# Layer 1's output product on float16 parts for 24 of 32 steps, with scales from squares summed ahead

## The chip, the cores and the metric

The kernel runs on one core of a Trainium2 chip. The core has TensorE (PE: matmuls, with weight loads shown apart as PEld), VectorE (DVE), ScalarE (ACT), GpSimd (POOL) and SyncE (SP, which here only issues DMAs). Each engine takes its instructions in order from its own queue; semaphores tie the queues together. DMAs are issued from the queues of SyncE, GpSimd and, rarely, ScalarE. The metric is the device time of one execution in microseconds, as the median of several runs.

## The reference

A two-layer transformer-like model on 256 tokens and 256 context tokens, width 2048, branch width 4096, all inputs float32:

```python
for i in range(2):
    shift, scale, gate = split(silu(c) @ ada_w[i] + ada_b[i])
    h  = rmsnorm(x)  * norm_g[i] * (1 + scale)   + shift      # 256 x 2048
    hc = rmsnorm(xc) * norm_g[i] * (1 + scale_c) + shift_c    # context rows
    y, yc = branch[i](h, hc)          # layer 0: Fourier mixer; layer 1: windowed attention
    x = x + gate * (y @ w_out[i])     # (256 x 4096) @ (4096 x 2048)
    if i == 0: xc = xc + gate_c * (yc @ w_out[0])
return rmsnorm(x) * final_g
```

Both branches end in a gate, `f * silu(z)` with `z = h @ w_z`. Layer 1's attention has 64 query heads of width 64 on 8 key/value heads, keys from a window of tokens and from the context. The product that is changed is layer 1's `y @ w_out[1]`, 256 x 4096 by 4096 x 2048.

## The kernel before, in words

**Products from parts.** Every large product is made of three matmuls (`mm3`, lines 144 to 147): each operand is split into a high and a low part, and high x high, high x low and low x high are added in PSUM. The parts have one of two types. On float32r parts, `split` (lines 65 to 67) lets ScalarE cast the source to the high part (L66) and VectorE, or GpSimd, subtract it from the source (L67). On float16 parts, `split16` (L137, L138) multiplies by a power of two first, so that the values fit float16; that scale comes from the sum of the squares of the whole operand (`sum_scale`), and the result is multiplied back by the inverse power. A weight half, 128 x 1024, takes two buffers of the pool `ws` (6 buffers of 4 KB) as float32r and one as float16.

**Layer 0.** After the Fourier mixer (up to about 320 us), z is made on float16 parts for all branch blocks (321 to 658 us, `z_out`). Then comes the output product of layer 0 (659 to 1001 us): 32 steps `i`, two passes (`sw`) over the output's halves with 16 weight tiles (`kg`) each; each step is 48 matmuls of 512 columns. Weights are the held operand, the branch parts stream. Weight tiles with `kg` below 14 use float16, the last two of a pass float32r. The branch parts are made by `y_split0(i + 1)` during step `i`, in the first pass only (the last two pairs in both passes); a float16 part takes the buffer of an earlier branch block, block 0's a buffer of the pool `act`. For the weights' scale, the whole of `w_out[0]` is read a second time ahead of its use, in 128 loads of 256 KB on GpSimd's queue into buffers of `act` (33 of 2 KB), which `scan_loads` issues (L824) and `scan_sums` squares on ScalarE (L817). At the same time VectorE makes the conditioning vectors that come later (`ada_jobs`, L796): a tile of 1 MB of `ada_w` per turn, one or two turns per step (`ada_rate`: two in steps 6 to 9 and 17 to 24). From the output product on, ada tiles and weight tiles share the three buffers of the pool `raw` (L50), loaded on SyncE's queue in the program's order.

**Layer 1.** A short stage ends layer 0 (norms, transposes, stores to `x1d`). The key/value product follows (1007 to 1103 us), on float32r parts, while ScalarE and VectorE make the parts `h1` and `h1c` of the normed rows. Then the attention runs in 66 slots `i` (about 7 us each), with two units of other work in each slot (`filler`, `emit_unit`): the query and z products (units "q" and "z") and at the end 12 units "o", the first 512 columns of the output product for steps k = 0 to 23. A slot has the scores and softmax of one pair of heads (`stage_s`: VectorE L1361 and L1377, ScalarE L1364 and L1376) and the value product of the pair two slots earlier (`stage_o`). Gated branch blocks land in `y1`, two blocks of 256 tokens to a tile (`emit_y`).

**Layer 1's output product.** Tokens are the held operand (two blocks of 128), weights stream 512 wide; 32 steps k. `w1_next` splits a weight half for the first 512 columns (`wo1a`), `y_split` the branch block (ScalarE casts, GpSimd subtracts for k below 24, VectorE above), four steps ahead of use. After the attention come steps 24 to 31 of these columns, then 1024 columns (`wo1b`, 16 tiles) and the last 512 (`wo1c`, 8 tiles). `evac` multiplies by the gate (`gbc`, a row spread over all partitions) and adds the residual, `finish` norms and stores.

**What sets the order.** The program is written once in the order of the loops; a planner then orders each engine's queue by that order and by when it thinks that operands and buffers are ready, so work of later steps runs ahead where its buffers are free. `tc.issue_after(ins)` holds what stands in its block behind `ins` on the same engine. `last_cast` and `last_sub` are the newest cast on ScalarE and subtraction on VectorE (or GpSimd).

## Time and profile before

| | |
|---|---|
| median of 3 runs | 1782.79 us (1778.72 to 1785.88) |
| profiled execution | 1780.77 us |
| its span, first to last instruction | 1779.0 us |
| mean granted TensorE clock | 0.997 |
| busy: PE, PEld, DVE, ACT, POOL | 98%, 69%, 78%, 60%, 16% |
| DMA | 438.74 MB, mean 247 GB/s |

Times in the rows are microseconds from the span's start. The page's second part cuts the span into 40 slices of 44.5 us, one digit each (9 is 90% busy or more). A row of a group by line is: line, engine, operation, tile written and tiles read, shape, count, then busy us and mean ns of one, then the engine's idle time just before such instructions with what ended it. A matmul's duration in the rows overlaps with the next one, so TensorE's pace is read from the count of matmuls in a stretch. In a timeline the bracket has the idle time before an instruction and what it waited for. For a DMA, "to landing" is the time from its issue to its end.

### The profile page before, as it was taken

What the parts mean: (1) busy time and instruction counts of PE and PEld (TensorE: products, weight loads), DVE (VectorE), ACT (ScalarE), POOL (GpSimd) and SP (SyncE); (2) the same over time, 40 slices, a digit from 0 to 9 for tenths busy, and PEclk for the clock granted to TensorE, in tenths of its full rate; (3) what the DMA queues carried; (4) which work ended last, traced back from release to release, by engine and by line L of the source; (5) the groups of instructions that cost most, each with busy time, mean ns of one, the idle gap of its engine ahead of it and who ended that gap; (6) DMA issues with size and microseconds to landing.
All of it is one profiled execution on the core that took longest, in us unless ns stands there. A gap on an engine that the chain in (4) does not pass through costs nothing. (4 is left out here: it accounts for less than half of the span.)

```text
span 1779.0 us, 26403 instructions
## 1 busy us (share of the span) xinstructions
PE 1740.9 (98%) x9517; PEld 1222.3 (69%) x9517; DVE 1392.8 (78%) x2401; ACT 1062.4 (60%) x1989; POOL 293.3 (16%) x368
## 2 busy tenths in 40 slices
PE   6999999999999999999999999999999999999997
PEld 4679999544444444446444888788878888887886
DVE  5779888797777778876885654899899999997455
ACT  5545556377767747544122533688788878896343
POOL 0002111212222132000000000412303230233010
PEclk9999999999999999999999999999999999999999
DMA  9998998778988989774775323588998897987543
GB/s 394 417 357 247 283 276 237 296 285 319 328 305 317 313 302 322 262 298 171 284 287 222 119 95 115 169 193 208 213 209 199 222 217 203 206 210 264 191 167 142
DMA packets 220962, 438.74 MB, mean 247 GB/s; under 512 B 154720, under 2 KB 155120, under 8 KB 189088
## 3 DMA queue, kind: packets, MB, share of 16 engines
q1 hardware_dynamic: 182784, 351.85, 61.0%
q0 software_dynamic: 33904, 78.25, 14.8%
q10 hardware_dynamic: 4144, 6.95, 1.1%
q8 instruction: 75, 1.23, 0.3%
q14 instruction: 55, 0.45, 0.1%
HBM read 391.91 MB, written 12.59 MB: 227 GB/s over the span
## 5 line engine op out<-in xcount | busy, mean ns | idle before, releaser
L67 DVE TENSOR_TENSOR wl<-raw,wh 128x1024 fp32r<-128x1024 f32 x213 | 282.0, 1329 | 144.5 <-ACT wh L66 129.8
L66 ACT CAST wh<-raw 128x1024 fp32r<-128x1024 f32 x213 | 222.4, 1045 | 177.4 <-PE ps L146 152.7
L146 PE MATMUL ps<-act,wf 128*128 128x512 f16 x512 | 194.0, 379 | 0.0
L145 PE MATMUL ps<-act,wf 128*128 128x512 f16 x512 | 189.8, 379 | 1.4 <-ACT act L864 0.7
L147 PE MATMUL ps<-act,wf 128*128 128x512 f16 x512 | 191.1, 379 | 0.0
L1323 PE MATMUL ps<-h,wh 128*128 128x512 f32 x512 | 184.8, 396 | 0.0
L145 PEld LDWEIGHTS <-wf 128*128 128x128 f16 x960 | 94.0, 98 | 118.0 <-ACT wf L137 7.9
L145 PE MATMUL ps<-y,wf 128*128 128x512 f16 x448 | 170.3, 381 | 3.5 <-ACT wf L137 3.5
L147 PEld LDWEIGHTS <-wf 128*128 128x128 f16 x960 | 93.9, 98 | 113.2 <-DVE wf L138 0.3
L146 PE MATMUL ps<-y,wf 128*128 128x512 f16 x448 | 170.8, 381 | 0.0
L146 PEld LDWEIGHTS <-wf 128*128 128x128 f16 x960 | 94.1, 98 | 109.5 <-issue 1.1
L147 PE MATMUL ps<-y,wf 128*128 128x512 f16 x448 | 164.4, 379 | 0.0
L137 ACT ACTIVATE wf<-raw,nrm 128x1024 f16<-128x1024 f32 x56 | 61.3, 1140 | 139.3 <-DMA raw<-in_wo 133.9
L1325 PE MATMUL ps<-h,wl 128*128 128x256 f32 x512 | 138.6, 281 | 0.0
L146 PE MATMUL ps<-wl,h 128*128 128x512 f32 x320 | 126.8, 396 | 0.2 <-DVE wl L67 0.2
L147 PE MATMUL ps<-wh,h 128*128 128x512 f32 x320 | 125.3, 395 | 0.0
L145 PE MATMUL ps<-wh,h 128*128 128x512 f32 x320 | 124.0, 402 | 0.0
L138 DVE SCALAR_TENSOR_TENSOR wf<-raw,tn,wf 128x1024 f16<-128x1024 f32 x64 | 79.8, 1282 | 42.5 <-ACT wf L137 42.4
L1377 DVE SCALAR_TENSOR_TENSOR f<-p,sm,f 128x512 f16<-128x512 f32 x128 | 105.7, 845 | 9.0 <-ACT f L1376 8.6
L1323 PEld LDWEIGHTS ps<-h,wh 128*128 128x128 f32 x512 | 96.3, 188 | 19.0
L1364 ACT ACTIVATE p<-ps,mx 128x512 f32<-128x512 f32 x128 | 87.9, 689 | 35.4 <-DVE mx L1361 30.6
L1376 ACT ACTIVATE f<-p,sm 128x512 f16<-128x512 f32 x128 | 87.6, 717 | 31.8 <-DMA ft<-f 12.9
(394 smaller groups left out, 4452.1 us busy)
## 6 DMA issues: line engine op xcount, KB each, us to landing
raw<-in_wz SPq DMA_DIRECT2D x64, 1024.0 KB, 5.4
raw<-in_adw SPq DMA_DIRECT2D x38, 1024.0 KB, 6.3
raw<-in_awp SPq DMA_DIRECT2D x32, 1024.0 KB, 12.7
act<-in_wo POOLq DMA_DIRECT2D x128, 256.0 KB, 7.2
raw<-in_wo SPq DMA_DIRECT2D x32, 1024.0 KB, 6.7
raw<-in_wq SPq DMA_DIRECT2D x32, 1024.0 KB, 5.2
raw<-in_wu SPq DMA_DIRECT2D x32, 1016.0 KB, 6.6
raw<-in_wo1b SPq DMA_DIRECT2D x16, 1024.0 KB, 4.9
```

Source lines behind the costliest of these rows:

```text
L66: last_cast[0] = S.copy(h, src).ins
L67: last_sub[0] = eng.tensor_tensor(l, src, h.bitcast(F32), op=ALU.subtract).ins
L137: last_cast[0] = S.activation(w[:, 0], src, AF.Copy, scale=up).ins
L138: last_sub[0] = V.scalar_tensor_tensor(w[:, 1], src, up, w[:, 0], op0=ALU.mult, op1=ALU.subtract).ins
L145: PE.matmul(o, wh, xh, start=start, stop=False)
L146: PE.matmul(o, wh, xl, start=False, stop=False)
L147: return PE.matmul(o, wl, xh, start=False, stop=stop).ins
L1323: PE.matmul(o[0], wh[:, q], hx1[k], start=k == 0, stop=k == KT - 1)
L1325: PE.matmul(o[0][:, 0:N], wl[:, q], hx1[k][:, 0:N], start=False, stop=False)
L1364: S.activation(pt[tb], so[tb], AF.Exp, bias=mx[:, tb : tb + 1], scale=-1.0, accum_out=sm[:, tb : tb + 1])
L1376: S.activation(f[:, 0:512], pt[tb], AF.Copy, scale=sm[:, tb : tb + 1])
L1377: V.scalar_tensor_tensor(f[:, 512:1024], pt[tb], sm[:, tb : tb + 1], f[:, 0:512], op0=ALU.mult, op1=ALU.subtract)
```

## The change

Layer 1's output product uses float16 parts for k = 0 to 23, all 2048 columns; k = 24 to 31 stay on float32r.

- The weights' squares: the 24 weight tiles concerned are read a second time in 48 halves. 22 halves are loaded in layer 0's output product from step 14 on (`scan_loads1`, two loads of 256 KB per half on GpSimd's queue into `act`; two halves a step, one in steps 17 to 24) and squared on ScalarE one step later, behind that step's weight casts (`scan_tops1`). 26 halves are loaded in the key/value product (`scan_loads2`, 512 KB each into four new buffers `pz`; four per weight tile, later three).
- The branch's squares: `y_sums` squares each finished tile of `y1` (12 tiles) on ScalarE two slots later. At slots 54 and 56 the sums are joined and the scales made (`out_sum`, `out_scale`).
- Splits: `w_half` makes float16 weight parts. `y_split` works on tiles of two blocks for k below 24: GpSimd multiplies by the scale, ScalarE casts, GpSimd subtracts. Blocks 24 to 31 are multiplied by both scales, so that the sums in PSUM fit together; ScalarE casts and VectorE subtracts, blocks 24 to 27 now inside the loop.
- `gbc` is multiplied by the inverse scale once.
- Layer 0: `y_split0(i + 1)` stands behind the newest weight cast on ScalarE and the newest subtraction on VectorE in all steps, and the ada turns behind the newest subtraction in all steps (before: steps 0, 1 and 12 to 18). The parts of block 1 take a buffer of `act` of their own too.

The diff, cut to its core:

```diff
+    def scan_tops1():
+        while pend:
+            t, c = pend.pop(0)
+            S.activation(t, t, AF.Square, accum_out=c)
+    def scan_loads1(n):
+        for j in [next(scans1) for _ in range(n)]:
+            for q in range(2):
+                t = act()
+                c = (j % 2 * 2 + q) * 512
+                nc.gpsimd.dma_start(t, w1s[j // 2][:, c : c + 512])
...
-                        t = (ypool if k else actp).tile([P, 1024], F16, tag="y" if k else "act", name="y")
+                        t = (ypool if k > 1 else actp).tile([P, 1024], F16, tag="y" if k > 1 else "act", name="y")
...
-            if sw == 0:
+            if i < 14:
...
+            elif i == 14:
+                with tc.issue_after(last_cast[0]):
+                    scan_sums()
+                scan_loads1(2)
+            elif 14 < i < 30:
+                with tc.issue_after(last_cast[0]):
+                    scan_tops1()
+                scan_loads1({i: 1 for i in range(17, 25)}.get(i, 2) if i < 29 else 0)
...
-                y_split0(i + 1)
+                with tc.issue_after(last_cast[0]), tc.issue_after(last_sub[0]):
+                    y_split0(i + 1)
...
-            with tc.issue_after(last_sub[0]) if i < 2 or 11 < i < 19 else nullcontext():
+            with tc.issue_after(last_sub[0]):
                 for _ in range(ada_rate.get(i, 1)):
                     next(ada)
...
+            def scan_loads2(n):
+                for j in [next(scans1) for _ in range(n)]:
+                    t = kvp.tile([P, 1024], F32, tag="pz", name="pz", bufs=4)
+                    nc.gpsimd.dma_start(t, w1s[j // 2][:, j % 2 * 1024 : j % 2 * 1024 + 1024])
+                    pend.append((t, scn[:, j - 22 : j - 21]))
...
+                with tc.issue_after(last_cast[0]):
+                    scan_tops1()
+                with tc.issue_after(pow_end[0]):
+                    scan_loads2(4 if kg < 2 else 3)
...
-                return half_split(raw1[0], n % 2)
+                return (w_half if n < 12 else half_split)(raw1[0], n % 2)
...
+                    S.activation(act(), y1[j], AF.Square, accum_out=g1[:, 2 + j : 3 + j])
...
+            def split16b(h, l, src, up):
+                last_cast[0] = S.activation(h, src, AF.Copy, scale=up).ins
+                last_sub[0] = V.scalar_tensor_tensor(l, src, up, h, op0=ALU.mult, op1=ALU.subtract).ins
...
             def y_split(k):
-                if 16 <= k < 24:
-                    t = act(F32R)
-                else:
-                    t = (h1p if k < 16 else fin[0]).tile([P, 512], F32R, ...)
-                split(t[:, 0:N], t[:, N : 2 * N], y1[k // 2][...], GP if k < 24 else V)
+                src = y1[k // 2]
+                if k < 24:
+                    t = h1p.tile([P, 1024], F16, tag="h1", name="ys", bufs=16)
+                    GP.tensor_tensor(src, src, uy.broadcast_to([P, 512]), op=ALU.mult)
+                    S.copy(t[:, 0:512], src)
+                    GP.tensor_tensor(t[:, 512:1024], src, t[:, 0:512], op=ALU.subtract)
+                    return
...
+            S.activation(gbc, gbc, AF.Copy, scale=dn1)
...
-                w = ws_split(raw(a["wo1b"][kg]))
+                w = [(w_half if kg < 12 else half_split)(t, i) for i in range(2)]
```

More of the change, by code (lines that the diff above doesn't have):

```diff
@@ L1030, in tile_dit @@
                     evac0(sw * 8 + b, o[b])
+    for c, q in ((0, slice(80, 108)), (15, slice(0, 16))):
+        V.tensor_reduce(g1[:, c : c + 1], scn[:, q], axis=AX.X, op=ALU.add)
     x1d = dram.tile([2, P, D], F32, name="x1d")
@@ new lines, in tile_dit, with y_sums, out_sum @@
+            ypairs, ynext = [], [0]
+            def y_sums(n, i):
+                while ynext[0] < min(n, len(ypairs)) and ypairs[ynext[0]] <= i - 2:
+                    j = ynext[0]
+                    ynext[0] += 1
+                    S.activation(act(), y1[j], AF.Square, accum_out=g1[:, 2 + j : 3 + j])
+            uw, uy, ub, dn1 = (g1[:, c : c + 1] for c in (20, 21, 22, 23))
+            def out_sum():
+                V.tensor_reduce(g1[:, 14:15], g1[:, 2:14], axis=AX.X, op=ALU.add)
```

59 lines of the change are left out of this document (49 added, 10 removed).

## The prediction

> **What bounds the kernel now.** I read the page's first two parts, then busy times by stage, then the groups by line.
>
> ```profile
> PE 1740.9 (98%) x9517; PEld 1222.3 (69%) x9517; DVE 1392.8 (78%) x2401; ACT 1062.4 (60%) x1989; POOL 293.3 (16%) x368
> PE   6999999999999999999999999999999999999997
> DVE  5779888797777778876885654899899999997455
> ```
>
> TensorE is busy in every slice from start to end, so a change pays only if TensorE needs less time per product or if one of its few gaps closes; and it costs as soon as another engine makes TensorE wait. VectorE is the only one that comes near, in the attention (slices 26 to 35). The busy time of each stretch (columns: us, then busy time and count of PE, PEld, DVE, ACT, POOL, then granted clock, DMA share, GB/s):
>
> ```profile
> 658.00:700.00 42.00, 42.00 (x196) 19.07 (x195) 34.78 (x52) 25.99 (x53) 13.47 (x25) 1.00 0.95 348
> 734.00:738.00 4.00, 4.00 (x11) 1.50 (x12) 4.00 (x6) 2.94 (x6) 0.54 (x1) 0.57 0.60 201
> 840.00:970.00 130.00, 130.00 (x604) 58.93 (x603) 108.70 (x164) 28.35 (x26) 1.07 (x2) 1.00 0.71 269
> 1010.00:1042.00 32.00, 32.00 (x138) 25.74 (x138) 29.73 (x63) 18.59 (x36) 0.00 (x0) 1.00 0.43 139
> 1042.00:1091.00 49.00, 49.00 (x211) 39.45 (x210) 10.91 (x10) 8.67 (x9) 0.00 (x0) 1.00 0.25 86
> 1156.00:1553.00 397.00, 395.73 (x2183) 329.43 (x2183) 370.65 (x685) 324.19 (x634) 87.25 (x63) 1.00 0.87 207
> 1553.00:1606.00 53.00, 52.60 (x280) 42.95 (x278) 50.19 (x97) 46.42 (x102) 16.77 (x17) 1.00 0.85 218
> 1606.00:1632.00 26.00, 22.97 (x134) 18.50 (x135) 19.62 (x30) 17.21 (x33) 11.91 (x18) 1.00 0.80 285
> 1636.00:1724.00 88.00, 88.00 (x381) 71.31 (x380) 41.04 (x36) 34.93 (x36) 4.22 (x2) 1.00 0.55 191
> ```
>
> 840 to 970 is layer 0's output product on float16 parts, 1636 to 1724 layer 1's on float32r parts. Both are gapless and all matmuls are 512 wide: 130.00 / 604 = 0.2152 us against 88.00 / 381 = 0.2310 us per matmul. That 0.0158 us is what the change is about.
>
> **The product itself (step 1).** 24 of 32 steps go to float16, each with 2 token blocks x 4 column blocks x 3 partial products: 576 matmuls x 0.0158 = 9.1 us less TensorE time. The 432 of the last 1536 columns run where VectorE (41.04 of 88) and ScalarE (34.93 of 88) have half their time free: 6.8 us, which I count in full. The casts there change little:
>
> ```profile
> L67 DVE TENSOR_TENSOR wl<-raw,wh 128x1024 fp32r<-128x1024 f32 x213 | 282.0, 1329 | 144.5 <-ACT wh L66 129.8
> L66 ACT CAST wh<-raw 128x1024 fp32r<-128x1024 f32 x213 | 222.4, 1045 | 177.4 <-PE ps L146 152.7
> L137 ACT ACTIVATE wf<-raw,nrm 128x1024 f16<-128x1024 f32 x56 | 61.3, 1140 | 139.3 <-DMA raw<-in_wo 133.9
> L138 DVE SCALAR_TENSOR_TENSOR wf<-raw,nrm,wf 128x1024 f16<-128x1024 f32 x56 | 70.0, 1283 | 22.6 <-ACT wf L137 22.3
> ```
>
> A weight half costs ScalarE 0.1 us more (1140 for 1045 ns) and VectorE 0.05 us less, and needs one buffer of the weight pool in place of two, so casts can run further ahead. No row has float16 tokens as the held operand and weights streaming 512 wide; the nearest is layer 0's product with the roles swapped. Bounds: 0 and 9.1 us.
>
> **The first 512 columns (step 2).** The other 144 matmuls (2.3 us) run in the last attention slots, within 1553 to 1632, mixed with softmax. Of 1553 to 1606 VectorE has 50.19 of 53 us taken, ScalarE 46.42. What the change moves: branch parts went to GpSimd as 24 subtractions of 256 columns; now 12 multiplications and 12 subtractions of 512.
>
> ```profile
> L1089 POOL TENSOR_TENSOR act<-act,rt 128x512 f32<-128x512 f32 x14 | 20.6, 1488 | 0.1
> L67 POOL TENSOR_TENSOR ys<-act,ys 128x256 fp32r<-128x256 f32 x16 | 16.3, 1052 | 43.2 <-ACT ys L66 43.2
> L67 POOL TENSOR_TENSOR act<-act 128x256 fp32r<-128x256 f32 x8 | 7.0, 911 | 18.3 <-ACT act L66 18.3
> ```
>
> 24 x 1.488 = 35.7 us for 16.3 + 7.0 = 23.3: 12.4 us more of GpSimd. It matters through VectorE, whose same instruction is slower while GpSimd works: the first row is from 1571 to 1587, where GpSimd subtracts, the second from 1588 to 1604, where it rests.
>
> ```profile
> L67 DVE TENSOR_TENSOR wl<-raw,wh 128x1024 fp32r<-128x1024 f32 x4 | 6.3, 1568 | 0.6 <-ACT wh L66 0.6
> L67 DVE TENSOR_TENSOR wl<-raw,wh 128x1024 fp32r<-128x1024 f32 x6 | 7.2, 1218 | 0.1
> ```
>
> That is 0.35 us per large instruction. Of VectorE's 97 instructions in 53 us I count half as large, one every 1.1 us or somewhat more, so 12.4 us of GpSimd meet some 10 of them: 3.5 us, plus the four parts of steps 24 to 27 that now come inside the loop (256 wide; by L138's 1283 ns for 1024 some 0.3 to 0.5 us each, 2 us). 5.5 us against 2.8 us idle would more than eat the 2.3 us. Against it: the multiplications need only the scale, known from slot 56, and lie ahead of the crowded slots; and from 1606 to 1632, where TensorE stands idle 3.0 us, GpSimd's 7.0 us of subtractions go. Bounds: 4 us lost, 4 us gained. I count a gain of 1.1 us, half of 2.3.
>
> **The branch parts of layer 0 (step 3).** One gap in layer 0's output product is long. TensorE first:
>
> ```profile
> 730.97 0.38 PE L147 MATMUL ps<-y,wf 128*128 128x512 f16 x1
> 734.00 0.61 PE L145 MATMUL ps<-y,wf 128*128 128x512 f16 x1 [2.66 <-ACT wf L137]
> ```
>
> ScalarE in the same microseconds (L882 is a branch part, L137 the weight cast), and SyncE's issue of these weights with its landing time:
>
> ```profile
> 732.19 0.72 ACT L882 ACTIVATE y<-y,nrm 128x512 f16<-128x512 f32 x1 [0.82 <-DVE y L883]
> 732.82 2.17 ACT L137 ACTIVATE wf<-raw,nrm 128x1024 f16<-128x1024 f32 x2
> 721.57 0.33 SPq L50 DMA_DIRECT2D raw<-in_wo  x1
> DMA to landing us min/median/max: 4.8/4.8/4.8
> ```
>
> The weights were issued at 721.57 and landed 4.8 us later, at 726.4. Their casts stood in ScalarE's queue behind branch parts, each waiting for VectorE, until 732.82. The change queues the parts behind the casts and, by one more separate buffer, breaks the chain in which each part waits for the one before. Then the cast ends near 729, ahead of 731.2. Gain: 2.66 us, and the clock: from 734 to 738 the granted clock was 0.57, 11 matmuls in 4.00 us where 11 x 0.2152 = 2.4, so 1.6 us more. Sum 4.3 us; bounds 0 (the next late weights take its place) and 4.3. Queued behind on ScalarE are then the parts themselves, needed a whole step (48 x 0.2152 = 10.3 us) later.
>
> The Trainium skill, "TensorE: Matmul & The Clock Gate", Part 1, has the clock halve only after a window of about 3.4 us without work; by that a gap of 2.66 us would cost itself alone, and the sum below would be 1.6 us smaller. Here the row shows a halved clock after 2.66 us, and I go by it.
>
> **The sums of squares (step 4).** 48 half tiles of 512 KB are read once more: 22 while layer 0's output product runs, as 44 loads on GpSimd's queue, 26 in the key/value product. ScalarE squares each:
>
> ```profile
> L817 ACT ACTIVATE act<-act 128x512 f32<-128x512 f32 x128 | 78.7, 616 | 0.0
> L817 ACT ACTIVATION_READ_ACCUMULATOR act<-act 128x1 f32 x128 | 24.1, 189 | 0.0
> L645 ACT ACTIVATE pz<-pz 128x1024 f32<-128x1024 f32 x12 | 12.8, 1064 | 3.5 <-DMA pz<-in_wz 3.5
> ```
>
> Layer 0: 44 x (0.616 + 0.189) = 44 x 0.8 = 35 us, where ScalarE has 28 of 130 us taken; hidden. Key/value: 26 x 1.25 = 33 us where it has 18.59 of 32 and 8.67 of 49; hidden, if the first four loads land before their squares stand in front of h. Its DMA (139 and 86 GB/s) has room for 13 MB. The attention gets 12 x 0.8 = 10 us on ScalarE over 397 us with 324 taken; hidden. For all of these together 0.5 us, bounds 0 and 3.
>
> What is not hidden is the DMA in the second half of layer 0's product, steps 17 to 24, two more 256 KB loads a step. There weights and two ada tiles a step share three raw buffers in SyncE's order (SyncE's issues, then ScalarE's cast of step 25, TensorE's first matmul on it, and who waited for that weight tile):
>
> ```profile
> 889.38 1.47 SPq L50 DMA_DIRECT2D raw<-in_adw  x2
> 900.29 1.47 SPq L50 DMA_DIRECT2D raw<-in_adw  x2
> 922.14 0.33 SPq L50 DMA_DIRECT2D raw<-in_adw  x1
> 922.27 2.19 ACT L137 ACTIVATE wf<-raw,nrm 128x1024 f16<-128x1024 f32 x2 [8.64 <-DMA raw<-in_wo]
> 924.44 0.38 PE L145 MATMUL ps<-y,wf 128*128 128x512 f16 x1
>   PEld L147: 0.3, 1
> ```
>
> The ring turns in 900.29 - 889.38 = 10.9 us (32.76 in three turns), TensorE's step is 10.3: the lead melts, and near 924 it is zero (a weight load waits 0.3 us for VectorE). Whatever the new loads add here, TensorE pays. How much a load can be slowed shows in the ada tiles' landing, first from 660 to 700, where layer 0's own scan is dense, then from 880 to 925, where there is none:
>
> ```profile
> DMA to landing us min/median/max: 7.8/9.2/9.7
> DMA to landing us min/median/max: 4.8/5.0/7.5
> ```
>
> 9.2 - 5.0 = 4.2 us with 25 loads in 42 us (POOL, first row of the stretches), 6 a step; two a step cost a third, 1.4 us, on a load they fully overlap. They are issued as ScalarE's squares free tiles, behind the weight cast, so they fall on the weights' load (1.4 us, once) and only on the end of the ada load that sets the ring (I take 0.17 us in each of 8 steps, 1.4 us): 2.8 us. Bounds: 0, and 8 x 1.4 = 11 us.
>
> **Small things (step 5).** The scale takes four one-column matmuls and five tiny VectorE steps at slot 56; the matmuls wait for a sum that was queued two slots earlier, and behind them on TensorE stand the scores of slot 56. I count nothing: the cover is those two slots, and if VectorE fell so far behind, the cost would be that lag. The gate row is scaled once by ScalarE, 2048 wide: twice L645's 1064 ns. From 1606 to 1632 ScalarE has 17.21 of 26 us taken, which covers it; but if the row is late, the weight casts queue behind it. 0.3 us. On GpSimd's queue the xT loads for the evacuations now stand behind the new loads; they are needed at steps 15 and 31 only, and I count nothing.
>
> **Sum.** The profiled execution took 1780.77 us, 2 us under the median of 1782.79 and inside 1778.72 to 1785.88; I make no allowance for that. 1780.8 - 6.8 - 1.1 - 4.3 + 2.8 + 0.5 + 0.3 = 1772.2. Prediction 1772 us.
>
> **The rivals.**
> *A, the ring decides (slower).* The new loads run ahead of their place as far as tiles are free, and bunch on the ada loads: 4.2 us in six of the eight steps, the first two paid by lead, is 25 us. 1780.8 - 12.2 + 25 + 0.8 = 1794. It turns the sign from 1.4 us per step in eight steps (11.4 us of gains). For it: zero lead at 924, and no buffer is added. Against it: the rate is two loads per step there, not six.
> *B, the attention's end is VectorE's.* Step 2 costs 4 us in place of 1.1 gained: 1777. For it: 50.19 of 53.
> *C, the tie brings nothing.* The change doesn't do what it says of layer 0, because with the chain gone the weights land late themselves (ada at two a step starts there): 1776.5.
> *D, GpSimd locks VectorE out.* 12.4 us of added GpSimd time stop VectorE fully instead of by 0.35 us per instruction, with 2.8 us idle to absorb it: 9.6 us lost in place of 1.1 gained, 1783. Against it: 1568 ns is not twice 1218. The Trainium skill, "SBUF — State Buffer", Who interferes with whom, says so of VectorE instructions with two SBUF inputs, which would be those rows; the trace shows them slowed by a third only.
>
> **How the numbers follow.** About 0.5%, 9 us, is what a measurement of this kernel can tell from no change: faster means below 1773.9, slower above 1791.7. Forecast 0.62, with its own range 1764 to 1776: 0.53 below 1773.9, 0.09 above. A 0.16, slower. B 0.10, C 0.08, D 0.04: within 0.5%. So faster 0.53, same 0.31, slower 0.16. Range 1763 to 1790: from all bounds on the good side (1780.8 - 9.1 - 4.3 - 4 = 1763) through B, C, D and the ring's full 1.4 us per step into the lower part of A.
>
> **What would show it.** Right: 0.215 us per matmul in 1636 to 1724 where 0.231 was; no gap before a cast near 730 and clock 1.00 there; short waits of TensorE for the weight casts between 880 and 930, 3 us in all; ScalarE's squares in the key/value product without a gap of TensorE. Wrong: waits of many us on the raw weights in layer 0's second half; TensorE waiting for VectorE or GpSimd parts in the last attention slots; a float16 matmul slower than 0.215 us with tokens held.

## The result and the profile after

The changed kernel took 1792.84 us in the median of 5 runs (1791.27 to 1796.61), the kernel before 1779.86 us on the same chip (1777.25 to 1785.88). The ratio is 1.0079, 95% interval 1.0057 to 1.0101: the change makes the kernel slower by 0.8%. The forecast was 1772 us, faster. The profiled execution, from which the rows of the changed kernel come, is the slowest of the five (1796.61 us).

The engines' busy time and the slices of the span, from the page of the changed kernel:

```profile
PE 1738.6 (97%) x9525; PEld 1172.3 (65%) x9525; DVE 1405.2 (78%) x2410; ACT 1126.5 (63%) x2142; POOL 344.8 (19%) x438
PE   6999999999999999999899999999999999988997
PEclk9999999999999999999999999999999999998999
```

TensorE's row had a 9 in every slice but the first and the last. Now, with slices of 44.9 us, it has an 8 in the 20th (852 to 897 us, layer 0's second half) and in the 36th and 37th (1570 to 1660, the attention's end), and in the last of these the granted clock falls as well. Those are the two places to look at. Busy times by stretch, in the columns of the prediction (us, then busy time and count of PE, PEld, DVE, ACT, POOL, clock, DMA share, GB/s):

```profile
728.00:734.00 6.00, 6.00 (x30) 2.74 (x28) 5.14 (x8) 4.64 (x8) 0.00 (x0) 1.00 0.92 352
840.00:910.00 70.00, 62.08 (x281) 27.10 (x280) 55.59 (x84) 20.48 (x36) 6.46 (x12) 0.98 0.89 322
1010.00:1097.00 87.00, 87.00 (x383) 70.46 (x384) 45.78 (x81) 59.11 (x106) 13.06 (x25) 1.00 0.77 275
1568.00:1606.00 38.00, 33.44 (x170) 21.66 (x169) 37.03 (x50) 32.31 (x60) 37.41 (x27) 0.96 0.56 148
1606.00:1640.00 34.00, 24.98 (x118) 12.89 (x116) 24.77 (x47) 17.82 (x35) 4.11 (x8) 0.85 0.95 273
1660.00:1700.00 40.00, 40.00 (x185) 19.26 (x184) 26.54 (x22) 22.32 (x22) 3.94 (x2) 1.00 0.63 219
```

The first row is the place of the old gap: gapless, clock 1.00. The second is the first bad place, 62.08 us busy of 70. The third is the key/value product with 26 of the new loads and squares in it, busy throughout. The fourth and fifth are the attention's end: GpSimd works 37.41 of 38 us, VectorE 37.03, TensorE loses 4.6 and then 9.0 us. The last is the product on float16: 40.00 / 185 = 0.2162 us per matmul, and 17 of these 185 are still float32r.

Where the difference arises, from the starts of the same matmuls in both traces (the columns are lengths in us, the last is what the changed kernel adds):

| stretch | before | after | |
|---|---|---|---|
| layer 0's product, steps 6 and 7 | 25.2 | 20.8 | -4.4 |
| the same, steps 19 to 24 | 62.2 | 72.6 | +10.4 |
| attention, scores of slot 23 to scores of slot 55 | 240.7 | 244.3 | +3.6 |
| scores of slot 55 to the last matmul of the first 512 columns | 83.5 | 96.6 | +13.1 |
| last 1536 columns | 133.5 | 127.5 | -6.0 |

With about -0.9 us between step 24 and slot 23 and a tenth or two ahead of step 6 and behind the last matmul, that is the 15.8 us between the spans of the two profiled executions (1779.0 and 1794.8). Slots are counted from 0, as `i` in the program; the expectation of e17 calls the same two scores those of slots 24 and 56. The fourth row is called the end stretch below, the second the ring stretch. Each length is from one execution: in e1 and e2, which leave this part of the program as it is, the third row is 244.7 and 243.6 us and the end stretch 95.7 and 95.2, so a difference of about 1 us in it says nothing.

**The first bad place.** SyncE's ada loads, then GpSimd's loads of the new sums with what released them, and two groups of waits between 850 and 925 us, ScalarE's and TensorE's (in total, times, the longest):

```profile
853.99 2.62 SPq L50 DMA_DIRECT2D raw<-in_adw  x2
865.34 2.62 SPq L50 DMA_DIRECT2D raw<-in_adw  x2
...
902.37 1.48 SPq L50 DMA_DIRECT2D raw<-in_adw  x2
```

```profile
859.92 1.15 POOL L841 DMA_DIRECT2D act<-in_wo1b  x2 [13.41 <-ACT act L834]
871.13 1.15 POOL L841 DMA_DIRECT2D act<-in_wo1b  x2 [10.06 <-ACT act L834]
```

```profile
ACT wf L137 <- DMA raw<-in_wo: 53.4, 6, 11.1
PE ps L145 <- ACT wf L137: 7.9, 5, 3.0
```

The ring turns in (902.37 - 853.99) / 4 = 12.1 us where it took 10.9, and TensorE's step is 10.4. TensorE waits for the weight cast, and the cast for the weights: the lead is used up by the third turn, and then each turn costs what it is longer.

**The second bad place.** TensorE's two long waits at the attention's end, and GpSimd in that time (L1260 multiplies a branch part, L1262 subtracts, L1542 loads the residual):

```profile
1589.39 0.38 PE L146 MATMUL ps<-wf,ys 128*128 128x512 f16 x1 [3.80 <-DVE wf L1249]
...
1620.39 0.37 PE L1479 MATMUL ps<-ft,v 128*128 128x256 f16 x1 [8.85 <-DMA ft<-f]
```

```profile
1568.59 16.99 POOL L1260 TENSOR_TENSOR act<-act,gt 128x512 f32<-128x512 f32 x12 [32.06 <-DVE gt L1243]
1585.55 19.34 POOL L1262 TENSOR_TENSOR ys<-act,ys 128x512 f16<-128x512 f32 x12
1604.83 4.36 POOL L1542 DMA_DIRECT2D act<-x1d  x8
```

GpSimd has no pause from 1568.59 to 1604.83: it can't begin before the scale is known (L1243, slot 56), and then does 24 instructions in a row. VectorE's groups in the same time (mean ns after the bar):

```profile
L1249 DVE SCALAR_TENSOR_TENSOR wf<-raw,gt,wf 128x1024 f16<-128x1024 f32 x6 | 11.3, 1917 | 0.0
L1446 DVE CUSTOM_DVE_ANT_0 ps<-ps,mask,nsink 128x512 f32<-128x512 f32 x8 | 5.8, 748 | 0.0
L1462 DVE SCALAR_TENSOR_TENSOR f<-p,sm,f 128x512 f16<-128x512 f32 x4 | 5.2, 1298 | 0.8 <-ACT f L1461 0.8
L67 DVE TENSOR_TENSOR wl<-raw,wh 128x1024 fp32r<-128x1024 f32 x3 | 4.5, 1515 | 0.0
L1451 DVE SCALAR_TENSOR_TENSOR sm<-sm,es 128x2 f32<-128x2 f32 x3 | 2.8, 920 | 0.0
L1268 DVE SCALAR_TENSOR_TENSOR ys<-act,gt,ys 128x256 fp32r<-128x256 f32 x2 | 2.7, 1377 | 0.0
L1244 DVE TENSOR_TENSOR gt<-gt 128x1 f32<-128x1 f32 x1 | 1.0, 1011 | 0.0
```

The 128x2 instruction of the softmax takes 920 ns and a 128x1 one 1011. In the kernel before, the first of these took 152 ns while GpSimd rested, so that can't be their own work. The experiments go after what it is.

### The profile page after: what moved, and what is told of

It is laid out like the page before. It is cut to its first block, busy times and chain, and to the rows that moved or that the text cites. A ratio compares the mean times of both kernels' runs of the same rounds, so it can differ in the third digit from the quotient of the medians.

```text
span 1794.8 us, 26703 instructions
## 1 busy us (share of the span) xinstructions
PE 1738.6 (97%) x9525; PEld 1172.3 (65%) x9525; DVE 1405.2 (78%) x2410; ACT 1126.5 (63%) x2142; POOL 344.8 (19%) x438
## 5 line engine op out<-in xcount | busy, mean ns | idle before, releaser
L67 DVE TENSOR_TENSOR wl<-raw,wh 128x1024 fp32r<-128x1024 f32 x167 | 217.4, 1303 | 103.3 <-ACT wh L66 77.7
L66 ACT CAST wh<-raw 128x1024 fp32r<-128x1024 f32 x167 | 174.1, 1043 | 99.8 <-PE ps L146 58.8
```

The costliest lines, as they stand in the source:

```text
L66: last_cast[0] = S.copy(h, src).ins
L67: last_sub[0] = eng.tensor_tensor(l, src, h.bitcast(F32), op=ALU.subtract).ins
```

## The experiments

My theory after the result: layer 0's loads make the ring late, and at the attention's end several things could: GpSimd's work beside VectorE, the residual's loads beside the softmax transposes (two of them landed after 12.75 and 11.30 us, with eight loads under way), or weight casts that run ahead of the softmax. The expectations stand as they were written ahead of each run. Each ratio is to the kernel before on the same chip; the changed kernel's was 1.0079.

**The ring: loads or order?** Both runs leave the 44 loads out of layer 0, the second keeps the squares. They differ from the changed kernel in these lines, first e1:

```diff
-                scan_loads1(2)
+                [next(scans1) for _ in range(22)]
...
-                scan_loads1({i: 1 for i in range(17, 25)}.get(i, 2) if i < 29 else 0)
+    V.memset(scn[:, 80:108], 0.5)
+    V.memset(scn[:, 0:16], 0.5)
```

> The changed kernel without the 44 loads and 44 squares in layer 0's output product; two constants stand in the columns of the sums, so the scale is not that of the weights. Theory 1 (the loads decide the ring): the five waits of TensorE for layer 0's weight casts between 858 and 908 us (8.7 us in all) go, the ada tiles turn in 10.9 us or less in place of 12.3, and the time comes down by 9 to 11 us, to about 1783. Rival (the tie does it: with each step's ada work queued behind the branch parts the raw buffers come free later, whether or not anything is loaded): the waits stay, and the time stays within 3 us of 1793.

Measured (e1): 1783.14 us, ratio 1.0016 (1.0005 to 1.0026). The ring stretch takes 62.2 us, to the tenth as before the change, and TensorE waits for no weight cast there. SyncE's ada loads in this run:

```profile
859.46 1.47 SPq L50 DMA_DIRECT2D raw<-in_adw  x2
...
903.44 1.47 SPq L50 DMA_DIRECT2D raw<-in_adw  x2
```

(903.44 - 859.46) / 4 = 11.0 us per turn. The tie, which is still in, has no part in the loss.

```diff
-            S.activation(t, t, AF.Square, accum_out=c)
+            S.activation(t if t is not None else act(), t if t is not None else r_bc, AF.Square, accum_out=c)
...
-                t = act()
...
-                nc.gpsimd.dma_start(t, w1s[j // 2][:, c : c + 512])
...
```

> The 44 squares of layer 0 stay in ScalarE's queue, but each reads a tile that lies in SBUF already; the 44 loads are left out, and constants stand in for the sums. If the loads' traffic on the DMA engines is what makes weights and ada tiles late, this comes out as the run without loads and squares, about 1783. If it is the squares between the weight casts on ScalarE (44 x 0.8 us), the waits of TensorE near 858 to 908 us stay and the time is about 1793.

Measured (e2): 1783.87 us, ratio 1.0023 (1.0012 to 1.0034), ring stretch 62.2 us. The squares on ScalarE cost nothing that these runs can tell; the loads do it.

**The attention's end, one suspect at a time.** First the residual's loads (tr_end is the newest softmax transpose):

```diff
...
-                    nc.gpsimd.dma_start(x2[tb][c], x1d[tb, :, c * 512 : (c + 1) * 512])
+                    with tc.issue_after(tr_end[0]):
+                        nc.sync.dma_start(x2[tb][c], x1d[tb, :, c * 512 : (c + 1) * 512])
```

> The changed kernel with its eight loads of the residual (256 KB each) issued on SyncE behind the last softmax transpose, in place of GpSimd as soon as tiles are free. Theory (these loads run at the same time as two softmax transposes, which then take 11 to 13 us to land in place of 3 to 5.5): the wait of 8.85 us near 1620 shrinks below 2 us, the slow clock after it goes, and the time comes down by 9 to 11 us, to about 1783. Rival (the transposes are late because VectorE and GpSimd are, the loads only happen to be there): the wait stays above 5 us and the time stays within 3 us of 1793.

Measured (e3): 1791.25 us, ratio 1.0064 (1.0042 to 1.0087). The wait for the transposes is 3.4 us (the groups of waits, 1555 to 1657), so the loads did hold them up, but the end stretch only goes from 96.6 to 92.7 us. The theory's time is missed by 8 us; the rival's time is met, its wait above 5 us is not; and the wait for the weight remainder stays.

```profile
PE ps L146 <- DVE wf L1250: 4.2, 3, 3.8
PE ps L1480 <- DMA ft<-f: 3.4, 1, 3.4
```

Then GpSimd's multiplications:

```diff
-                    GP.tensor_tensor(src, src, uy.broadcast_to([P, 512]), op=ALU.mult)
```

> The changed kernel with the 12 multiplications of the branch parts on GpSimd left out (17 us of GpSimd; the first 24 parts are then not scaled, so that much of the product has another factor). Theory (GpSimd slows VectorE, my forecast's 0.35 us per large instruction being too little: 1.9 us for 1.28 us were seen): VectorE's remainder instructions come back to about 1.3 us from 1568 to 1585, the wait of 3.8 us near 1585 goes, and the time comes down by 4 to 8 us, to 1785 to 1789. Rival (GpSimd runs beside VectorE): within 3 us of 1793.

Measured (e4): 1794.74 us, ratio 1.0076 (1.0051 to 1.0102); end stretch 95.8 us, as in the runs that change nothing here. The 3.8 us wait shrinks to 1.3, as the theory said, and the time does not:

```profile
PE ps L1478 <- DMA ft<-f: 12.6, 1, 12.6
...
PE ps L146 <- DVE wf L1249: 1.9, 2, 1.3
```

Counted from the scores of slot 55, TensorE came to the softmax 5 us sooner and then stood there 12.6 us. Half of GpSimd's work removed moves the wait, it doesn't shorten the stretch.

Then the order on VectorE, by fewer buffers and by an explicit order (f_end is the softmax remainder of the same slot):

```diff
-                w = wsp.tile([P, 2, 1024], F16, tag="ws", name="wf")
+                w = [wsp.tile([P, 2, 1024], F16, tag="ws", name="wf") for _ in range(2)]
...
```

> The changed kernel with the two float16 parts of a weight half in two buffers of the weight pool in place of one, so that casts can run ahead no further than float32r casts do; nothing else changes. Theory (the casts run ahead of the softmax: from 1587 to 1606 us VectorE spends some 14 us on weight remainders, and the remainder of the softmax of slot 60 waits for them): the wait of 9 us near 1620 falls below 4 us, the last attention matmul comes 5 to 12 us earlier and the time is 1781 to 1788. Rival (the buffers do not matter, GpSimd's contention and the loads do): within 3 us of 1793.

Measured (e5): 1792.7 us, ratio 1.0064 (1.0041 to 1.0088); end stretch 93.5 us. The softmax came 13 us earlier (scores of slot 61), the wait near 1620 fell to 0.51 us, and TensorE waited 9.2 us for weight remainders, where it had waited 4.3. The wait did what the theory said, the time did not.

```diff
-                return (w_half if n < 12 else half_split)(raw1[0], n % 2)
+                with tc.issue_after(f_end[0]):
+                    return (w_half if n < 12 else half_split)(raw1[0], n % 2)
```

> The changed kernel; the remainders of layer 1's weight halves in the attention's last slots are queued on VectorE behind the softmax remainders of their own slot (buffers as in the changed kernel). Theory (order on VectorE): the softmax of slots 59 to 61 comes early again, its transposes are issued before the residual's loads, the wait near 1620 falls below 4 us, time 1781 to 1788. Rival (VectorE simply has too much to do there): the wait moves to the weight casts, TensorE waits for them as long as it did for the softmax, and the time stays within 3 us of 1793.

Measured (e6): 1800.12 us, ratio 1.0107 (1.0081 to 1.0133); end stretch 103.0 us. The rival was right, and more than right: with the remainders last, TensorE waited 7.3 us for one of them.

> As the run before, with the residual's eight loads behind the last softmax transpose as well. If the order on VectorE and the loads are two separate causes, it is 2 to 6 us below that run; if the loads only hurt because the transposes were late, the two are equal within 2 us.

(Its edit is the two before together.) Measured (e7): 1794.49 us, ratio 1.0082 (1.0059 to 1.0105), 5.6 us below the run before, end stretch 99.1 us. The loads matter by some 4 us here too, and the order still loses. So neither the loads nor the order is the root: whichever goes first on VectorE, the other is late.

**All of GpSimd's work away.**

```diff
-                    GP.tensor_tensor(src, src, uy.broadcast_to([P, 512]), op=ALU.mult)
...
-                    GP.tensor_tensor(t[:, 512:1024], src, t[:, 0:512], op=ALU.subtract)
...
```

> The changed kernel without any of GpSimd's 24 instructions on the branch parts (multiplications and subtractions; the high part stands in for the remainder, unscaled, so that part of the product is another number). Theory (GpSimd holds VectorE out: an instruction of VectorE with two SBUF inputs waits for the GpSimd instruction under way, some 0.65 to 0.95 us whatever its size): between 1568 and 1606 us every remainder takes 1.28 us, every softmax remainder 0.75 us, VectorE is not full, TensorE's waits at the attention's end come down from 21 us in all to 5 or less, and the time is 1776 to 1782. Rival (VectorE has too much work there even alone, or the order is at fault): waits above 10 us stay, and the time stays above 1786.

Measured (e9): 1783.3 us, ratio 1.0018 (1.0003 to 1.0033); end stretch 80.3 us, 16.3 less, and no wait of TensorE in it above 2 us, with the loads, the buffers and the order rules of the changed kernel. The time is 1 us above what the theory expected, and not all of the 16.3 us is gain: slots 23 to 55 take 247.6 us here, 3.3 more than in the changed kernel, which no run explains. VectorE's same groups from 1568 to 1605 in this run:

```profile
L1249 DVE SCALAR_TENSOR_TENSOR wf<-raw,gt,wf 128x1024 f16<-128x1024 f32 x10 | 12.6, 1280 | 0.0
L1444 DVE CUSTOM_DVE_ANT_0 ps<-ps,mask,nsink 128x512 f32<-128x512 f32 x9 | 6.6, 755 | 0.4 <-PE ps L1443 0.3
L67 DVE TENSOR_TENSOR wl<-raw,wh 128x1024 fp32r<-128x1024 f32 x4 | 4.9, 1222 | 0.5 <-ACT wh L66 0.5
L1460 DVE SCALAR_TENSOR_TENSOR f<-p,sm,f 128x512 f16<-128x512 f32 x6 | 4.5, 748 | 0.8 <-ACT f L1459 0.8
L1266 DVE SCALAR_TENSOR_TENSOR ys<-act,gt,ys 128x256 fp32r<-128x256 f32 x4 | 1.8, 482 | 1.4 <-ACT ys L1265 1.4
...
L1449 DVE SCALAR_TENSOR_TENSOR sm<-sm,es 128x2 f32<-128x2 f32 x4 | 0.6, 154 | 1.2 <-ACT es L1448 1.2
...
L1244 DVE TENSOR_TENSOR gt<-gt 128x1 f32<-128x1 f32 x1 | 0.2, 152 | 0.0
```

Row against row: 1917 to 1280, 1298 to 748, 1515 to 1222, 920 to 154, 1377 to 482, 1011 to 152 ns. For most forms the extra is 0.55 to 0.9 us, whatever the size of the instruction. The mask step, whose scores lie in PSUM, does not change (748 and 755). With the counts of the changed kernel (6, 4, 3, 3, 2, 1) these six groups alone lost 3.8 + 2.2 + 0.9 + 2.3 + 1.8 + 0.9 = 11.9 us of VectorE in 37 us.

Is it a wait for the GpSimd instruction under way, or a shared rate? Cutting GpSimd's instructions in four tells:

```diff
+                    cut = [slice(c, c + 128) for c in range(0, 512, 128)]
+                    for q in cut:
+                        GP.tensor_tensor(src[:, q], src[:, q], uy.broadcast_to([P, 128]), op=ALU.mult)
```

(and the subtraction alike).

> The changed kernel with each of GpSimd's 24 instructions on the branch parts cut in four of 128 columns; the work is the same. Theory (a VectorE instruction with two SBUF inputs waits until the GpSimd instruction under way has ended): the extra time falls with the length of GpSimd's instruction, so the softmax's 2-element sums (0.92 us beside GpSimd, 0.15 without) come to 0.3 to 0.5 us and the weight remainders to about 1.5 us, TensorE's waits at the attention's end fall from 21 us to 8 to 14, and the time is 1782 to 1788. Rival (both engines share a bandwidth, so only GpSimd's busy time counts): remainders stay at 1.9 us and the time within 3 us of 1793.

The groups from 1568 to 1605:

```profile
L1262 POOL TENSOR_TENSOR act<-act,gt 128x128 f32<-128x128 f32 x48 | 26.8, 595 | 32.3 <-DVE gt L1243 32.3
L1249 DVE SCALAR_TENSOR_TENSOR wf<-raw,gt,wf 128x1024 f16<-128x1024 f32 x6 | 8.6, 1451 | 3.8 <-ACT wf L1248 3.8
L1265 POOL TENSOR_TENSOR ys<-act,ys 128x128 f16<-128x128 f32 x10 | 7.1, 745 | 0.0
...
L147 PE MATMUL ps<-wf,ys 128*128 128x512 f16 x7 | 3.4, 488 | 8.3 <-POOL ys L1265 8.3
...
L1454 DVE SCALAR_TENSOR_TENSOR sm<-sm,es 128x2 f32<-128x2 f32 x3 | 0.9, 298 | 0.2 <-ACT es L1453 0.2
```

VectorE did as the theory said: 298 ns for the sums, 1451 for the remainders, extras of 0.14 and 0.17 us in place of 0.77 and 0.64, although GpSimd is busy for 33.5 of the 37 us. A shared rate, by which only GpSimd's busy time counts, is out. The time is another matter. It is 1799.78 us in the median (e13), ratio 1.0112 (1.0073 to 1.0151), where I had expected 1782 to 1788; but the four runs lie far apart (1790.77, 1793.01, 1806.56, 1807.1), so it can't be told from the changed kernel's, and the rows are from the slowest of them. There a quarter costs GpSimd 0.595 us where the whole cost 16.99 / 12 = 1.42, so its work grows from 36.3 us to 58.4, and TensorE waits 8.3 us for the parts themselves and 13.9 us for softmax transposes.

**Can the work be put elsewhere?** First only earlier: the scale is taken from the first 7 pairs of blocks at slot 36, and the multiplications run in slots 40 to 56 (with the residual's loads late).

```diff
-                    GP.tensor_tensor(src, src, uy.broadcast_to([P, 512]), op=ALU.mult)
...
+                y_sums(7, i)
+                if i == 38:
+                    one_scale(1, (14,))
+                if i > 39:
+                    y_muls(i)
```

> The changed kernel with the branch's scale taken from the first 7 pairs of blocks at slot 36, with two more binary places of room, so that its 12 multiplications run on GpSimd through slots 40 to 56, where it is mostly idle; and the residual's loads behind the last softmax transpose. If the multiplications' place and the loads are the two causes, TensorE's waits at the attention's end fall from 21 to below 8 us and the time is 1779 to 1784. If the order on VectorE (weight remainders ahead of the softmax) is the third and binds alone, they stay above 12 us, and the time is 1787 to 1791.

Measured (e10): 1795.92 us, ratio 1.0082 (1.0065 to 1.01); end stretch 92.8, no shorter than with the late loads alone (e3: 92.7), and slots 23 to 55 take 249.2 us in place of 244.3. Nine of the twelve multiplications run in a row from 1433 to 1446 us, and TensorE loses 4 of the 36 us from 1447 on.

(The next has the edit of e5 beside.)

> As the run before, and the float16 parts of a weight half in two buffers in place of one, so that remainders cannot run so far ahead. If the order binds in the run before, this one is 4 us or more below it; otherwise they are equal within 2 us.

Measured (e11): 1792.7 us, ratio 1.007 (1.0051 to 1.0089), end stretch 88.0 us: 4.8 below the run before in the trace, 3 in the time. That is in between; the order does cost something beside the subtractions that are left.

And with the loads moved as well:

> As the run before, and the sums of squares moved out of steps 17 to 24 of layer 0: two halves in each of steps 14 and 15, three in 16 and in 25 to 28, 29 in the key/value product; nothing is left out. Expected from the run without layer 0's loads: 10 us below the run before; with the tie's gain that is 1766 to 1774, ratio 0.992 to 0.996 to the kernel before. If 29 halves are too many for the key/value product, TensorE waits there between 1010 and 1090 us and half of it is lost.

```diff
-                scan_loads1({i: 1 for i in range(17, 25)}.get(i, 2) if i < 29 else 0)
+                scan_loads1({15: 2, 16: 3, 25: 3, 26: 3, 27: 3, 28: 3}.get(i, 0))
-                    scan_loads2(4 if kg < 2 else 3)
+                    scan_loads2(4 if kg < 5 else 3)
```

Measured (e12): 1785.81 us, ratio 1.0027 (1.0017 to 1.0038). The ring stretch is 64.2 us and the key/value product holds 29 halves without a gap, so moving the loads gives back 8.4 of the 10.4 us there, and 7 us of the time; I had expected 10, and a time below the kernel before.

Then the branch parts on ScalarE and VectorE, with nothing on GpSimd:

```diff
-                    GP.tensor_tensor(src, src, uy.broadcast_to([P, 512]), op=ALU.mult)
-                    S.copy(t[:, 0:512], src)
-                    GP.tensor_tensor(t[:, 512:1024], src, t[:, 0:512], op=ALU.subtract)
+                    split16b(t[:, 0:512], t[:, 512:1024], src, uy)
```

> The changed kernel with the branch parts of the first 24 steps formed as those of layer 0 are: ScalarE scales and rounds, VectorE forms the remainder, GpSimd does nothing there; nothing is left out. VectorE gets 12 x 0.75 = 9 us more and loses the waits for GpSimd (0.65 to 0.9 us for each of some 17 instructions from 1568 to 1605, 13 us). Expected 1783 to 1788: as the run without GpSimd's instructions, and up to 5 us more where VectorE's 9 us show. If GpSimd's relief is worth its price, it is 1793 or more.

Measured (e14): 1787.69 us, ratio 1.0053 (1.0036 to 1.007), as expected; end stretch 87.3 us, 9.3 less than with GpSimd. In the same 37 us VectorE makes all twelve parts and eight weight remainders, where the changed kernel had six:

```profile
L1249 DVE SCALAR_TENSOR_TENSOR wf<-raw,gt,wf 128x1024 f16<-128x1024 f32 x8 | 10.0, 1273 | 0.0
L1249 DVE SCALAR_TENSOR_TENSOR ys<-act,gt,ys 128x512 f16<-128x512 f32 x12 | 8.3, 742 | 0.0
```

So 8.3 us of work of its own were cheaper for VectorE here than GpSimd's help.

With the loads moved as in e12:

> As the run before, and the sums of squares out of steps 17 to 24 of layer 0 as in the run with all moved; nothing is left out, the scale is again taken from all 12 pairs at slot 56. The two causes found are then both away. Expected: 8 us below the run before, 1774 to 1780, ratio 0.996 to 0.9995 to the kernel before. If it stays above 1783, there is a third cause that no run has touched.

Measured (e15): 1781.72 us, ratio 1.001 (0.9997 to 1.0023); ring stretch 63.5, end stretch 88.8 us. That is 6 us below the run before, 2 more than expected at the upper end. And with the two buffers of e5 beside:

> As the run before, with two buffers for the float16 parts of a weight half. If remainders that run ahead of the softmax still cost something without GpSimd's work, this is 2 us or more below; if the longer lead helps, as much above.

Measured (e16): 1778.63 us, ratio 0.9995 (0.9982 to 1.0009); ring stretch 63.6, end stretch 83.7 us, against 62.2 and 83.5 before the change. The 3 us between the two runs point to remainders that run ahead of the softmax as a cost without GpSimd too. So the losses of these two stretches can be taken back, and what is left is a float16 product that gains nothing measurable: the tie and the last columns bring 4.4 + 5.6 us, the ring keeps 1.4 of them, and from the first scores to those of slot 55 it takes 421.0 us in place of 414.4. Those 6.6 us have no cause shown.

**The tie alone.** The kernel before with the three edits of layer 0's parts:

```diff
-                        t = (ypool if k else actp).tile([P, 1024], F16, tag="y" if k else "act", name="y")
+                        t = (ypool if k > 1 else actp).tile([P, 1024], F16, tag="y" if k > 1 else "act", name="y")
-                y_split0(i + 1)
+                with tc.issue_after(last_cast[0]), tc.issue_after(last_sub[0]):
+                    y_split0(i + 1)
-            with tc.issue_after(last_sub[0]) if i < 2 or 11 < i < 19 else nullcontext():
+            with tc.issue_after(last_sub[0]):
```

> The kernel before with the edits of layer 0's branch parts alone: both parts of a step queued behind the weight casts, ada work always behind them, one more separate buffer; no float16 in layer 1, no sums of squares. Theory (step 3 of my forecast): the gap of 2.66 us before 734 and the slow clock after it go, 4.3 us, and the time is 4 to 5 us under the kernel before, ratio 0.9975. Rival (the tie makes the ada tiles late): the ring's waits between 858 and 908 us show here too, and the ratio is 1.000 or more.

Measured (e8): 1774.45 us, ratio 0.9963 (0.9949 to 0.9977). That is 6.5 us under the kernel before, a little more than expected, and the fastest kernel of the study. The gap is gone (728 to 740 us):

```profile
728.00:740.00 12.00, 12.00 (x58) 5.44 (x56) 10.58 (x15) 7.13 (x15) 0.00 (x0) 1.00 0.86 311
```

Steps 6 and 7 take 20.8 us for 25.2, the ring stretch 62.2.

**The middle of the attention.**

```diff
-                    S.activation(act(), y1[j], AF.Square, accum_out=g1[:, 2 + j : 3 + j])
...
+                V.memset(g1[:, 2:14], 100.0)
```

> The changed kernel without the 12 sums of squares of the branch on ScalarE in the attention (a constant stands in their columns). From the first scores of slot 24 to those of slot 56 the changed kernel takes 244.3 us, the kernel before 240.7. Theory (the squares, 10 us of ScalarE, are not hidden as I had counted them): the stretch comes back to 240.7 to 241.5 us. Rival (they are hidden; the other order of the queues, or the tiles they take, costs it): it stays above 243 us. The whole time falls by no more than 4 us.

Measured (e17): 1791.37 us, ratio 1.0075 (1.0051 to 1.0099). Slots 23 to 55 take 242.8 us, between the two expectations and below the 243.6 to 245.4 of the changed kernel and e1 to e7; slots 0 to 55 come from 417.8 to 413.8, where the kernel before takes 414.4. The squares look like a part of this loss, 1.5 us of the 3.6 by the one stretch and all of it by the other, but one execution of each doesn't settle 2 us. It stays open.

## Why the prediction was wrong

| step of the prediction | forecast | trace |
|---|---|---|
| 1, last 1536 columns | -6.8 | -6.0 |
| 2, first 512 columns, attention's end | -1.1 (bounds 4 either way) | +13.1 |
| 3, the tie | -4.3 | -4.4 |
| 4, layer 0's loads in the ring | +2.8 (bounds 0 and 11) | +10.4 |
| 4, squares in the key/value product and the attention | +0.5 (to 3) | 0 and, in slots 23 to 55 with all causes, +3.6 |
| 5, small things | +0.3 | +0.2 behind the last matmul, the rest not apart |

*Step 1 was right.* Tokens held and weights streaming cost what the swapped roles cost: with the 17 float32r matmuls at 0.2310, the other 168 of the 185 shown come to (40.00 - 3.93) / 168 = 0.2147 us.

*Step 3 was right* in place and size, and in the queueing. I had the cast end near 729; it only begins at 728.92, because the weights themselves land then, later than the 726.4 of before:

```profile
728.92 2.19 ACT L137 ACTIVATE wf<-raw,nrm 128x1024 f16<-128x1024 f32 x2 [4.70 <-DMA raw<-in_wo]
```

Step 7, in which the clock was 0.57 before, went from 12.0 to 10.4 us, which is the 1.6 us I had put down to the clock. Both halves are cast by 731.1, and TensorE has no gap. The tie alone confirms the gain. Rival C, by which the late weights eat it, falls, though the weights did come later.

*Step 4 failed in the term of the ring.* I had the right bound, 8 x 1.4 = 11 us, and then took 0.17 of the 1.4, because the new loads would be issued behind the weight cast and so "fall on the weights' load (1.4 us, once)". They start there, GpSimd issuing at 859.92 and SyncE the weights at 860.52, but they don't end there. Between 858 and 909 us the weights landed after 7.4 to 9.7 us (before: 6.1 to 7.5), and the ada loads of 860 to 906 us after 7.2 in the median (before: 5.8). The three buffers turn in one order: a load that lands later frees its buffer later, and the next load is issued later. So the turn was longer by 1.2 us, not by 0.17. The runs e1 and e2 show that it is the loads and not the squares or the tie; how the delay passes from buffer to buffer is read from the order of the issues, not tested. Rival A had this mechanism and the sign, but took 4.2 us a turn where 1.2 were measured, and its 1794 comes near the result by luck: the other loss made up for it. The squares in the key/value product were hidden as said: TensorE busy 87.00 of 87.00, and they waited for data 2.6 us once (the operations of that line, idle before them):

```profile
L834 ACT ACTIVATE pz<-pz x26: 1042/1044/1064, 1018.4 to 1095.2; 128x1024 f32<-128x1024 f32 x26
...
  DMA pz<-in_wo1c: 2.6, 1
```

*Step 2 failed, and cost most.* The sentence that fell is "That is 0.35 us per large instruction ... 12.4 us of GpSimd meet some 10 of them: 3.5 us". Three things were wrong in it. The slowing is no share of VectorE's instruction: it is nearly the same for 128x2 as for 128x1024, as a wait for the GpSimd instruction under way would be, and I had counted the large ones only. It grows with GpSimd's instruction (e13), and these went from 256 to 512 columns (about 1.0 to 1.4 and 1.6 us). And it is not the 12.4 us added that count but all 36, since none of it can begin before the scale is known at slot 56, while the old subtractions left VectorE 1588 to 1604 free and had their last 7 us behind that. So the prediction's "lie ahead of the crowded slots" was wrong too. GpSimd in the kernel before:

```profile
1571.64 15.56 POOL L67 TENSOR_TENSOR ys<-act,ys 128x256 fp32r<-128x256 f32 x15 [0.92 <-ACT ys L66]
1605.52 4.24 POOL L67 TENSOR_TENSOR act<-act 128x256 fp32r<-128x256 f32 x4 [18.32 <-ACT act L66]
```

The trace of before had the row that shows it; I looked only at the large group. With GpSimd at work (1571 to 1587) and resting (1588 to 1604), in the kernel before:

```profile
L1366 DVE SCALAR_TENSOR_TENSOR sm<-sm,es 128x2 f32<-128x2 f32 x2 | 1.1, 553 | 0.2 <-ACT es L1365 0.2
```

```profile
L1366 DVE SCALAR_TENSOR_TENSOR sm<-sm,es 128x2 f32<-128x2 f32 x3 | 0.5, 152 | 0.0
```

0.40 us more on two elements is about the same as 0.35 on 1024: nearly a constant. Rival D named the mechanism and got 0.04, because I held "1568 ns is not twice 1218" against it. That was the wrong test, since the extra time goes by the other engine's instruction. The Trainium skill, "SBUF — State Buffer", Who interferes with whom, says that VectorE instructions with two SBUF inputs contend with GpSimd instructions that read SBUF, and those with at most one, outside the 2-port perf modes, do not. By that rule every remainder and every softmax sum pays and the mask step on PSUM does not; the trace agrees, with 920 against 154 ns for the one and 748 against 755 for the other.

What came on top followed it: the softmax was late, so its transposes were issued at 1606.71 and 1609.05, into the residual's loads. In the kernel before those loads were issued from 1609.7 on, behind the last transpose. I had named the relief of GpSimd from 1606 on, and not asked what its earlier end would start. The runs e3 to e7 show that this collision is worth 3.9 us of the stretch, the buffers 3.1 (step 1 had counted casts that run further ahead as a help), and that the order moves the wait about; e9 shows that without GpSimd's work the stretch is 80.3 us, 3.2 below the kernel before. But its slots 23 to 55 took 6.9 us more than the kernel before's, so no run shows the 2.3 us of step 2 as a gain of the whole.

*Step 5* was not measured apart; from the last matmul to the end the changed kernel takes 0.2 us more, where I had put down 0.3.

## What to carry to other kernels

Before work is given to GpSimd as a helper, compare VectorE's smallest two-input instructions with GpSimd at work and at rest: if they differ by much, every two-input instruction may be paying (here 0.4 us each beside subtractions of 1 us, 0.8 beside instructions of 1.4 to 1.6), and the help may cost more than the work. In a ring of buffers that is as long as the step, count added loads in every turn, not once: here two loads of 256 KB cost 1.2 us a turn, and most of that came back when they were moved to stages with slack. And of a change in several parts, measure the small one alone: here the tie of a few lines was worth 0.4%, and the large part nothing.

## What the hardware did that I had not expected

VectorE instructions of 128x2 and 128x1 took 0.92 and 1.01 us beside GpSimd instructions of 1.4 to 1.6 us, the first of them 0.30 beside ones of 0.6 to 0.75; without them both take 0.15. The extra falls faster than GpSimd's length, which no run explains.

Two softmax transposes of 12 us beside eight loads of 256 KB; from 1555 us on they took 3.1 to 5.8 in the kernel before, and the two at the same place in e3, with the loads moved, still 7.3 and 6.4. The issues from 1604 to 1610 with their median time to landing:

```profile
act<-x1d POOLq DMA_DIRECT2D x8, 256.0 KB, 9.6
...
ft<-f SPq DMA_TRANSPOSE x2, 12.0
```

Two loads of 256 KB lengthened the ring's turn by 1.2 us, that is 0.52 MB / 1.2 us = 437 GB/s. The fastest slices between 850 and 912 us in the kernel before moved 423 to 439 GB/s, so the loads cost about what their bytes take at the rate of the fastest slices, though the engines moved 287 GB/s on the mean. That this is the reason was not tested.

```profile
GB/s 328 381 370 222 74 296 418 423 370 391 69 58 296 423 428 428 386 11 69 248 412 407 423 418 69 0 217 423 418 439 428 106 0 211 433 418 428 428 122 0
DMA packets 2444, 17.80 MB, mean 287 GB/s; under 512 B 274, under 2 KB 274, under 8 KB 274
```
